# Pinning the VectorE sums of the modulation in the second to fourth token group of one encoder layer

## The chip, the cores and the metric

One Trainium2 chip, one of its cores. The metric is the device time of one execution in microseconds (us); lower is better. The time of a kernel is the median of several executions. A profile is one further execution, with its own time, recorded instruction by instruction. Five engines of the core work side by side, each on its own list of instructions in a fixed order: PE (TensorE, the matmuls), DVE (VectorE), ACT (ScalarE), POOL (GpSimd) and SP (SyncE), which here does nothing but issue DMAs. An engine that reaches an instruction whose input is not there waits, and all that stands behind it in its list waits too.

## The reference, cut to what matters

A layer of a streaming encoder runs over 2048 prompt tokens and 64 sample tokens of width 1024. Each of the two has its own conditioning vector, and the modulation `mod` is a product of that vector with a large weight:

```
mod = (c_act @ w_ada + b_ada)[:, None, :]
sh1, sc1, gt1, sh2, sc2, gt2 = jnp.split(mod, 6, -1)
h = rmsnorm(x, g1) * (1 + sc1) + sh1
proj = h @ w_in
...
hs, C, n, m = mlstm_seq(q..., k..., v..., ig, lf, C, n, m)
...
x = x + gt1 * mix
h2 = rmsnorm(x, g2) * (1 + sc2) + sh2
...
x = x + gt2 * ((jax.nn.silu(g) * a) @ w_down)
```

`sh2`, `sc2` and `gt2` (parts 3, 4 and 5 of the six) are wanted only after the mixer stage, so the kernel computes them in its background. This change concerns that background work.

## The kernel before

All inputs are float32. Where a full product is wanted, a number is split into a high and a low part, and three matmul passes replace one; the split weights of the first group are kept in memory (`hl_kept`) and loaded again by the later groups, 512 KB at a time.

The program has two stages. The first, about 0 to 740 us, is the mixer: four token groups of 512 tokens, the last with the 64 sample tokens besides. The second is the gated MLP in three groups of 704. For each of the four groups the mixer does this. `proj_v` (matmuls at L1141) makes V and the gates. `gate_rows` copies the gates out of PSUM (`gt`), transposes them on PE (L1184, L1185), and runs a chain of small rows over DVE and ACT: z, its absolute value, an Exp and an Ln on ACT, a log-sigmoid `lf`, two scans, then R and `RHL`. PE transposes these (L1238), DVE copies the result out as `CL`, PE multiplies (L1251), DVE copies out `GL`. Four heads follow, here hd0 to hd3. Each is three products q, k and the output gate th (`gemm`, matmuls at L492) and `lstm`: the decay factors (L1293) and their Exp on ACT (`at`), the transposes of k (L1306) that DVE multiplies into `kw`, the product of q and k (L1316) that DVE multiplies into `at`, the products of V with `kw` (L1331), which DVE adds into the states `st`, the cells (L1351, L1353), and `nd`. The stage ends with pooling (`poolmix`) and the output product (`outproj`).

Behind this lies background work that a generator hands out in small pieces between matmuls (`tick`):

- `ada(m, first)` (L191 to L228) computes one part of the modulation as plain sums on DVE. It has 16 steps. A step takes one 256 KB piece of `w_ada`, loaded by SP (L208) into a `raw` buffer, and adds it, multiplied by a column of the conditioning, into two rows of sums: one instruction for the prompt and one for the sample (L222 for the first of eight steps, L224 for the others). The sums are called `u` and `s` for the first eight steps and `s` and `acc` for the last eight. The load of step i+3 is issued when step i is done. The `raw` buffers are five in a ring, shared with the loads of other weights. `ada(2, True)` runs in the first group, and parts 3, 4 and 5 run in the second, third and fourth group with `first` false.
- `ada_end` (L230) finishes a part: a matmul (L234), a copy (L236), transposes (L240).
- `up_sums` prepares weights of the MLP: loads of `w_up` (L865), four DVE additions (L884, L885, L888, L889), a store of `wsum` (L875).
- `norm1` squares and adds the inputs of the next group (L930); `norm_h` makes the inputs of the MLP (L745 on DVE, L748 on ACT, load of `x2d` L758).

The order in each engine's list is not that of the source. A scheduler takes instructions that are ready in its own reckoning, by priority and by the place at which they were traced, so an instruction can float ahead of others that were traced before it. Two things bind it. Work called urgent (`gate_rows`, `lstm`, `poolmix`, and the splitting of weights at L425 and L428) has a raised priority. And `tc.keep_in_program_order(x)` pins an instruction: it may not stand ahead of what was traced before it on its engine. `up_sums` is pinned so in DVE's list and in SP's; the `w_ada` loads of the first group are pinned in SP's; the DVE steps of `ada` are not pinned at all.

Of the kernel before, what the change touches and what calls it, by code (L numbers as in the profile page):

```python
# [12 lines left out]
ALU = mybir.AluOpType  # L13
# [52 lines left out]
def tile_layer(ctx: ExitStack, tc: tile.TileContext, xT, vecs, cst, rst, w_mod, w_ada, w_qkou, w_v, w_pool,  # L66
               w_out, w_up, w_down, w_quad, st_C, st_pool, yT, o_pool, o_C, o_m, o_conv):
    nc = tc.nc
    act, dve, pool, pe = nc.scalar, nc.vector, nc.gpsimd, nc.tensor
# [105 lines left out]
    CA = cp.tile([P, KD, 2], F32, tag="CA", name="CA")  # L175
# [6 lines left out]
    def raw_tile():  # L182
        return wp.tile([P, WN], F32, tag="raw", name="raw", bufs=RB)
# [7 lines left out]
    def ada(m, first):  # L191


        todo = [(j, k) for j in range(2) for k in range(KD)]
        src = [w_ada[m - 2, k, :, j * 512:(j + 1) * 512] for j, k in todo]
        got = {}

        def load(i):
            if first:

                if i % 2 == 0 and i < len(todo):
                    w = a1.tile([P, 4, 256], F32, tag="w4", name="w4", bufs=4).rearrange("p (a b) c -> p a (b c)", a=2)
                    for d in range(2):
                        got[i + d] = w[:, d]
                        tc.keep_in_program_order(nc.sync.dma_start(out=w[:, d], in_=src[i + d]))
            elif i < len(todo):
                got[i] = raw_tile()[:, :512]
                nc.sync.dma_start(out=got[i], in_=src[i])  # L208
        lead = 4 if first else 3
        for i in range(lead):  # L210
            load(i)
        yield
        accs = []
        for i, (j, k) in enumerate(todo):
            if k == 0:

                acc = [a1.tile([P, UE], F32, tag=nm, name=nm)[:, :512] for nm in (("u", "s1"), ("s2", "acc"))[j]]
                accs += acc
            w = got.pop(i)
            for s in range(2):  # L220
                if k == 0:
                    dve.tensor_scalar(out=acc[s], in0=w, scalar1=CA[:, k, s:s + 1], scalar2=None, op0=ALU.mult)  # L222
                else:
                    dve.scalar_tensor_tensor(out=acc[s], in0=w, scalar=CA[:, k, s:s + 1], in1=acc[s],  # L224
                                             op0=ALU.mult, op1=ALU.add)
            load(i + lead)
            yield
        side.append(ada_end(m, accs))  # L228

    def ada_end(m, accs):  # L230

        pt = m2_ps()
        for c, acc in enumerate(accs):
            pe.matmul(pt[32 * c:32 * c + 32, :], ones[:, 0:32], acc, start=True, stop=True)  # L234
        MR = scr()
        dve.tensor_copy(MR[:, :512], pt)  # L236
        yield
        pt = m2_ps()
        for n in range(4):
            pe.transpose(pt[:, n * P:(n + 1) * P], MR[:, n * P:(n + 1) * P], ident)  # L240
        for j in range(2):
            bia = V[:, V_BA + m * 8 + 4 * j:V_BA + m * 8 + 4 * j + 4]
            dve.tensor_tensor(out=MOD[:, m, 4 * j:4 * j + 4],
                              in0=pt.rearrange("p (n c t) -> p n c t", n=4, c=4)[:, :, 2 * j:2 * j + 2, 0],
                              in1=bia.unsqueeze(2).broadcast_to([P, 4, 2]), op=ALU.add)
        if m == 4:
            scale_cols(G2, V_G2, 4, 0, KD)
# [139 lines left out]
    class Unit:  # L387

        state = 0
        w = raw = None  # L390
# [462 lines left out]
    if True:  # L853
# [604 lines left out]
        for o in groups:  # L1458
# [3 lines left out]
            if o.g > 0:  # L1462
                bg[3].append(ada(2 + o.g, False))
# [15 lines left out]
            if o.g == 0:  # L1479
                bg[3].append(ada(2, True))  # L1480
# [888 lines left out]
```

## Time and profile before

| what | us |
| --- | --- |
| median of 3 runs | 2169.86 |
| lowest and highest run | 2167.97, 2170.21 |
| the profiled execution | 2173.9 |
| its span, first to last instruction | 2172.1 |
| PE busy in the span | 2146.8 |
| DVE busy | 1663.1 |
| ACT busy | 1103.8 |
| PE busy in the first 800 us | 785.60 |
| the mixer of the second, third, fourth group begins at about | 205, 385, 566 |

In the views a row names an engine, a line of the program, an operation and its output and inputs (`out<-in`). A bracket holds the time for which the engine stood idle just before, and what ended that idle time. A view of waits adds these up by pair.

### The profile page before, as it was taken

The numbers are of one execution on the slowest core, as the hardware profiler recorded it, in microseconds if no ns is written. First come the engines' busy times: TensorE is split into PE (matmuls) and PEld (weight loads), VectorE is DVE, ScalarE is ACT, GpSimd is POOL, SyncE is SP. The second block draws the span as 40 slices with busy tenths as digits, with TensorE's granted clock in tenths as the row PEclk, the third lists the DMA queues.
The fourth block names the chain that finished last, engine by engine and source line by source line (L and its number), as shares of the span: only waits on it lengthen the run. The fifth ranks groups of instructions, "written<-read, shape, count | busy, mean of one in ns | idle before, by whom it ended". The sixth has DMA issues, their size and how long they took to land.

```text
span 2172.1 us, 38106 instructions
## 1 busy us (share of the span) xinstructions
PE 2146.8 (99%) x13529; PEld 2040.5 (94%) x13529; DVE 1663.1 (77%) x3107; ACT 1103.8 (51%) x2201; POOL 247.1 (11%) x468
## 2 busy tenths in 40 slices
PE   8999999999999999999999999999999999999998
PEld 7888888888899999999999999999999999999998
DVE  5768669767965778797968668888888797887874
ACT  4544335234333446464736445655656454565554
POOL 0000000001000201010101220100101121111112
PEclk9999999999999999999999999999999999999999
DMA  8986997997988477888969966666666875555542
GB/s 319 331 299 225 321 335 235 302 317 240 301 288 290 169 261 239 282 291 297 353 226 320 320 243 221 236 206 212 228 217 229 282 276 186 172 175 191 172 159 77
DMA packets 302439, 545.28 MB, mean 251 GB/s; under 512 B 25984, under 2 KB 118656, under 8 KB 302248
## 3 DMA queue, kind: packets, MB, share of 16 engines
q1 hardware_dynamic: 291656, 517.64, 70.3%
q10 hardware_dynamic: 10592, 25.20, 3.0%
q8 instruction: 107, 1.75, 0.3%
q14 instruction: 84, 0.69, 0.1%
HBM read 414.65 MB, written 128.08 MB: 250 GB/s over the span
## 4 chain that ended last, share of the span: by engine, by line
PE 84%; DMA 6%; DVE 5%; issue 2%; ACT 2%; SPq 0%; POOL 0%; DVEq 0%; ACTq 0%; POOLq 0%
PE mm L1602 35%; PE mm L492 21%; PE mm L2210 10%; PE mm L2071 9%; PE mm L1141 3%; DMA wt<-wsum 1%; DVE wt L428 1%; PE m L1331 1%; DMA hl_kept<-wt 1%; PE m L1316 1%; PE m L1351 1%; PE m L1353 1%; DMA raw<-w_ada 1%; DMA raw<-w_qkou 0%; DMA wsum<-w 0%
## 5 line engine op out<-in xcount | busy, mean ns | idle before, releaser
L1602 PE MATMUL mm<-hx,wt 128*128 128x352 f32 x5544 | 887.6, 321 | 1.1 <-DVE wt L428 0.7
L1602 PEld LDWEIGHTS mm<-hx,wt 128*128 128x128 f32 x5544 | 879.9, 188 | 3.6 <-DVE wt L428 2.4
L492 PE MATMUL mm<-hl,wt 128*128 128x512 f32 (+2 forms) x1920 | 385.4, 356 | 0.0
L425 ACT ACTIVATE wt<-raw 128x512 fp32r<-128x512 f32 (+3 forms) x468 | 275.9, 597 | 194.4 <-PE mm L492 56.1
L492 PEld LDWEIGHTS mm<-hl,wt 128*128 128x128 f32 x1920 | 314.7, 188 | 47.3 <-issue 4.4
L428 DVE TENSOR_TENSOR wt<-raw,wt 128x512 fp32r<-128x512 f32 (+3 forms) x468 | 306.9, 662 | 58.6 <-ACT wt L425 58.1
L2071 PE MATMUL mm<-av,wt 128*128 128x352 f32 x1512 | 248.2, 323 | 1.8 <-DVE x L2040 0.7
L2071 PEld LDWEIGHTS mm<-av,wt 128*128 128x128 f32 x1512 | 242.3, 188 | 5.1 <-DVE ea L1611 3.1
L2040 DVE SCALAR_TENSOR_TENSOR x<-mm,MOD,x 128x352 f32<-128x352 f32 (+5 forms) x384 | 180.1, 507 | 69.0 <-PE mm L2210 54.1
L2210 PE MATMUL mm<-av,wt 128*128 128x448 f32 (+1 forms) x1440 | 232.2, 322 | 0.0
L2210 PEld LDWEIGHTS mm<-av,wt 128*128 128x128 f32 x1440 | 221.1, 188 | 9.9
L1650 ACT ACTIVATE mm<-mm 128x352 f32<-128x352 f32 x204 | 91.4, 448 | 231.6 <-PE mm L1602 171.5
L492 PE MATMUL mm<-mx,wt 128*128 128x512 f32 (+1 forms) x960 | 182.9, 352 | 0.3 <-DVE scr L264 0.3
L492 PEld LDWEIGHTS mm<-mx,wt 128*128 128x128 f32 x960 | 159.4, 188 | 23.0 <-PE mm L492 0.5
L1580 DVE SCALAR_TENSOR_TENSOR ta<-ea,V,ta 128x704 f32<-128x704 f32 (+1 forms) x132 | 125.6, 951 | 54.1 <-ACT ta L1575 48.6
L1580 DVE SCALAR_TENSOR_TENSOR tg<-eg,V,tg 128x704 f32<-128x704 f32 (+1 forms) x132 | 125.6, 952 | 49.9 <-ACT tg L1575 47.3
L428 DVE TENSOR_TENSOR wt<-wt 128x512 fp32r<-128x512 f32 x204 | 138.1, 682 | 12.2 <-ACT wt L425 12.2
L425 ACT ACTIVATE wt<-wt 128x512 fp32r<-128x512 f32 x204 | 123.6, 622 | 37.4 <-DMA wt<-wsum 34.7
L1558 POOL COPY ea<-UC 128x2 f32<-128x2 f32 x66 | 33.0, 500 | 510.1 <-DVE ta L1580 428.7
L1799 ACT ACTIVATE tg<-tg 128x704 f32<-128x704 f32 (+1 forms) x66 | 52.4, 794 | 69.1 <-DVE tg L1580 69.0
L1141 PE MATMUL mm<-wt,hl 128*128 128x256 f32 (+1 forms) x576 | 71.2, 284 | 0.0
L1141 PEld LDWEIGHTS mm<-wt,hl 128*128 128x128 f32 x576 | 70.2, 189 | 0.8 <-issue 0.6
(306 smaller groups left out, 2214.6 us busy)
## 6 DMA issues: line engine op xcount, KB each, us to landing
wt<-wsplit SPq DMA_DIRECT2D x132, 512.0 KB, 4.3
raw<-w_up SPq DMA_DIRECT2D x198, 256.0 KB, 4.1
wt<-hl_kept SPq DMA_DIRECT2D x96, 512.0 KB, 5.8
wt<-wsum SPq DMA_DIRECT2D x132, 256.0 KB, 5.0
wsplit<-wt SPq DMA_DIRECT2D x66, 512.0 KB, 5.2
w<-w_up SPq DMA_DIRECT2D x88, 256.0 KB, 4.4
wsum<-w SPq DMA_DIRECT2D x44, 512.0 KB, 5.3
Bd<-fscr ACTq DMA_DIRECT2D x56, 352.0 KB, 4.2
```

What stands on the lines that cost most here:

```text
L425: act.activation(u.w[:, 0, :u.n], u.raw[:, :u.n], AF.Copy)
L428: dve.tensor_tensor(out=u.w[:, 1, :u.n], in0=u.raw[:, :u.n], in1=u.w[:, 0, :u.n].bitcast(F32), op=ALU.subtract)
L492: pe.matmul(ps[bi][:, :hi - lo], U[:, a, k % 4 * P:(k % 4 + 1) * P], mv[k][:, b, lo:hi], start=(at == 0 and pi == 0), stop=(k == order[-1] ...
L1141: pe.matmul(ps[ti][:n, :cols], h[4 * kh + k4][:, b, lo:lo + n], U[:, a, k4 % 2 * cols:(k4 % 2 + 1) * cols], start=(kh == 0 and k4 == 0 and ...
L1558: pool.tensor_copy(ext[:, 0:2], UC[:, f, :])
L1580: dve.scalar_tensor_tensor(out=t[:, :E], in0=ext[:, j:j + E], scalar=wc(j, f), in1=t[:, :E], op0=ALU.mult, op1=ALU.add)
L1602: pe.matmul(bk.t[:, :FH], U[:, a, kc * P:(kc + 1) * P], Bo.at(nm, kc, b), start=(first and kc == 0 and pi == 0), stop=(kc == 3 and pi == 2 ...
L1650: act.activation(to.t[:, :FH], bk.t[:, :FH], AF.Copy)
L1799: act.activation(self.tg[:, :E], self.tg[:, :E], AF.Silu)
L2040: dve.scalar_tensor_tensor(out=x3[n][:, a:b], in0=bk.t[:, a - lo:b - lo], scalar=gt2(n, s), in1=x3[n][:, a:b], op0=ALU.mult, op1=ALU.add)
L2071: pe.matmul(bk.t[:, :FH], U[:, a, c:c + P], quad.put(op, m, b), start=(first and m == 0 and pi == 0), stop=(m == 1 and pi == 2), skip_grou ...
L2210: pe.matmul(bks[i].t[:, :hi - lo], U[:, a, k % 4 * P:(k % 4 + 1) * P], av[k][:, b, lo:hi], start=(k == 0 and (a, b) == PASSES[0]), stop=(k ...
```

## The change

After it, each of the two DVE instructions of a step is pinned where `first` is false. That is 96 instructions, 32 in each of the three groups. No instruction is added or removed on any engine.

```diff
             for s in range(2):
                 if k == 0:
-                    dve.tensor_scalar(out=acc[s], in0=w, scalar1=CA[:, k, s:s + 1], scalar2=None, op0=ALU.mult)
+                    step = dve.tensor_scalar(out=acc[s], in0=w, scalar1=CA[:, k, s:s + 1], scalar2=None, op0=ALU.mult)
                 else:
-                    dve.scalar_tensor_tensor(out=acc[s], in0=w, scalar=CA[:, k, s:s + 1], in1=acc[s],
-                                             op0=ALU.mult, op1=ALU.add)
+                    step = dve.scalar_tensor_tensor(out=acc[s], in0=w, scalar=CA[:, k, s:s + 1], in1=acc[s],
+                                                    op0=ALU.mult, op1=ALU.add)
+                if not first:
+                    tc.keep_in_program_order(step)
             load(i + lead)
```

The lists of PE and POOL stay as they were, word for word. Those of DVE, SP and ACT change; in the pieces below lines behind L226 carry a number higher by two after the change.

**DVE, third group, hd0.** The rows from `CL` to `kw` before, with steps of `ada` (`s_4620`, `acc`) and of `up_sums` (`w_4688`) between them:

```order
L224 TENSOR_SCALAR acc<-raw,CA,acc 128x512
L264 COPY CL<-m_4557 128x4x4
L554 TENSOR_SCALAR RS_121<-m_4566 128x4
L224 TENSOR_SCALAR s_4620<-raw,CA,s_4620 128x512
L224 TENSOR_SCALAR acc<-raw,CA,acc 128x512
L264 COPY GL<-m_4614 128x16
L884 TENSOR_TENSOR w_4688<-w_4688 128x256
L224 TENSOR_SCALAR s_4620<-raw,CA,s_4620 128x512
L885 TENSOR_TENSOR w_4688<-w_4688 128x256
L224 TENSOR_SCALAR acc<-raw,CA,acc 128x512
L888 TENSOR_TENSOR w_4688<-w_4688 128x256
L264 TENSOR_TENSOR kw<-m_4647,CL 128x512
```

and the same place after:

```order
L266 COPY CL<-m_4557 128x4x4
L556 TENSOR_SCALAR RS_121<-m_4566 128x4
L224 TENSOR_SCALAR u<-raw,CA,u 128x512
L224 TENSOR_SCALAR s_4347<-raw,CA,s_4347 128x512
L886 TENSOR_TENSOR w_4492<-w_4492 128x256
...
L891 TENSOR_TENSOR w_4492<-w_4492 128x256
L224 TENSOR_SCALAR u<-raw,CA,u 128x512
L224 TENSOR_SCALAR s_4347<-raw,CA,s_4347 128x512
L266 COPY GL<-m_4614 128x16
L222 TENSOR_SCALAR s_4620<-raw,CA 128x512
L222 TENSOR_SCALAR acc<-raw,CA 128x512
L266 TENSOR_TENSOR kw<-m_4647,CL 128x512
```

Between `CL` and `kw` stood the thirteenth and fourteenth step before (each `s_4620` with `acc`), and there stand the seventh, eighth and ninth now.

**DVE, second group, hd1.** The last rows between the `nd` of hd0 and the `kw` of hd1, before:

```order
L930 TENSOR_TENSOR ssum<-ssum,mx_2640 128x512
L885 TENSOR_TENSOR w_2791<-w_2791 128x256
L224 TENSOR_SCALAR s_2810<-raw,CA,s_2810 128x512
L888 TENSOR_TENSOR w_2791<-w_2791 128x256
L224 TENSOR_SCALAR acc<-raw,CA,acc 128x512
L889 TENSOR_TENSOR w_2791<-w_2791 128x256
L930 TENSOR_TENSOR ssum<-ssum,mx_2640 128x512
L224 TENSOR_SCALAR s_2810<-raw,CA,s_2810 128x512
L224 TENSOR_SCALAR acc<-raw,CA,acc 128x512
L264 TENSOR_TENSOR kw<-m_3053,CL 128x512
```

and after:

```order
L224 TENSOR_SCALAR acc<-raw,CA,acc 128x512
L224 TENSOR_SCALAR s_2810<-raw,CA,s_2810 128x512
L224 TENSOR_SCALAR acc<-raw,CA,acc 128x512
L886 TENSOR_TENSOR w_2880<-w_2880 128x256
L932 TENSOR_TENSOR ssum<-ssum,mx_2640 128x512
L887 TENSOR_TENSOR w_2880<-w_2880 128x256
L890 TENSOR_TENSOR w_2880<-w_2880 128x256
L891 TENSOR_TENSOR w_2880<-w_2880 128x256
L224 TENSOR_SCALAR s_2810<-raw,CA,s_2810 128x512
L224 TENSOR_SCALAR acc<-raw,CA,acc 128x512
L224 TENSOR_SCALAR s_2810<-raw,CA,s_2810 128x512
L266 TENSOR_TENSOR kw<-m_3053,CL 128x512
```

In all there stand 4 instructions of `ada` and 4 of `up_sums` (and 3 of L930) between the two before, and 9, 8 and 3 now. The third group has the same numbers after the change, with none of `ada` before.

**SP, third group, the loads around hd0.** Before:

```order
L409 DMA wt<-hl_kept 128x2x512
L865 DMA w_4688<-w_up 128x2x256 x2
L208 DMA raw<-w_ada 128x512 x2
L409 DMA wt<-hl_kept 128x2x512 x2
L865 DMA w_4773<-w_up 128x2x256 x2
L208 DMA raw<-w_ada 128x512 x2
L409 DMA wt<-hl_kept 128x2x512 x3
L875 DMA wsum<-w_4539 512x1x256
```

and after:

```order
L867 DMA w_4601<-w_up 128x2x256 x2
L208 DMA raw<-w_ada 128x512
L867 DMA w_4688<-w_up 128x2x256
L208 DMA raw<-w_ada 128x512
L867 DMA w_4688<-w_up 128x2x256
L877 DMA wsum<-w_4492 512x1x256
L208 DMA raw<-w_ada 128x512 x2
L411 DMA wt<-hl_kept 128x2x512 x2
L867 DMA w_4773<-w_up 128x2x256 x2
L411 DMA wt<-hl_kept 128x2x512
```

A `w_ada` load whose buffer an earlier step must give back now stands nearer to the `hl_kept` loads that PE's weights come from. In the fourth group 15 of the 16 steps stood ahead of z before; after, the first stands in the end of `outproj`, and the rest behind z, on to hd1, so that the loads of `x2d` and the L745 and L748 rows change places there as well.

## The prediction

> **What bounds the kernel now.** The page comes first: its top and the row of PE.
>
> ```profile
> span 2172.1 us, 38106 instructions
> PE 2146.8 (99%) x13529; PEld 2040.5 (94%) x13529; DVE 1663.1 (77%) x3107; ACT 1103.8 (51%) x2201; POOL 247.1 (11%) x468
> ```
>
> PE works in 2146.8 of 2172.1 us. A change that only reorders DVE, ACT and SP can win no more than the idle time of PE that they cause where it acts, and can lose whatever new idle time it makes. So I asked the view of waits for PE, for the stretch from the second to the fourth group (190 to 740 us). It has two rows, each with what PE waited for, the sum, the count and the longest. The third row here is the longest of the whole execution.
>
> ```profile
> PE m L1331 <- DVE kw L264: 2.0, 1, 2.0
> PE m L1316 <- ACT at L264: 1.5, 1, 1.5
> PE m L1040 <- DMA mx<-xT: 5.7, 1, 5.7
> ```
>
> The first two are all that PE loses in those 550 us: 2.0 + 1.5 = 3.5 us, and that is the most that the change can win. The third lies at the very start, before PE's first matmul. Behind 740 us the lists of PE, DVE and SP are the same, and PE there only shifts with what came before.
>
> Next, the windows by stage (busy time and count of each engine, granted clock, DMA share, GB/s), to see how much room the other resources have:
>
> ```profile
> 260.00:320.00 60.00, 60.00 (x322) 50.61 (x321) 41.20 (x102) 20.29 (x64) 3.62 (x4) 1.00 0.97 336
> 390.00:440.00 50.00, 48.43 (x323) 43.59 (x321) 34.93 (x69) 14.54 (x29) 1.01 (x1) 1.00 0.95 325
> 440.00:500.00 60.00, 59.62 (x320) 50.38 (x321) 38.63 (x97) 20.71 (x64) 3.50 (x4) 1.00 0.91 305
> 605.00:660.00 55.00, 55.00 (x414) 52.45 (x413) 33.27 (x91) 20.76 (x62) 3.92 (x5) 1.00 0.87 282
> ```
>
> PE is full in each but for the 1.95 us around 440. DVE has a quarter to a third of its time free, so its sum is not the question, only the order in it. The DMA engines are nearly full (0.97 in hd0 and hd1 of the second group): a load that is issued late will land late.
>
> **The stall that the change touches.** Around 440 us the timeline of DVE and PE (start, length, instruction, and in brackets the idle time before it with its releaser):
>
> ```profile
> 429.69 0.75 DVE L224 SCALAR_TENSOR_TENSOR s<-raw,CA,s 128x512 f32<-128x512 f32 x1 [4.59 <-DMA raw<-w_ada]
> 431.02 0.17 DVE L264 COPY CL<-m 128x16 f32<-128x16 f32 x1
> 435.81 0.75 DVE L224 SCALAR_TENSOR_TENSOR s<-raw,CA,s 128x512 f32<-128x512 f32 x1 [4.55 <-DMA raw<-w_ada]
> 436.47 0.75 DVE L224 SCALAR_TENSOR_TENSOR acc<-raw,CA,acc 128x512 f32<-128x512 f32 x1
> 437.14 0.17 DVE L264 COPY GL<-m 128x16 f32<-128x16 f32 x1
> 439.55 0.68 DVE L264 TENSOR_TENSOR kw<-m,CL 128x512 f32<-128x512 f32 x1
> 440.38 1.13 PE L1331 MATMUL m<-va,kw 128*128 128x129 f32 x8 [1.95 <-DVE kw L264]
> 436.24 0.60 PE L1306 MATMUL m<-V,k 128*128 128x128 f32 x4
> ```
>
> Two steps of the sums, floated ahead of `CL` and `GL`, wait 4.59 and 4.55 us for their piece of `w_ada`, and hold DVE with them. `GL` comes at 437.14, five more rows follow, and `kw` starts at 439.55, though its input (L1306, 436.24 + 0.60) was there at 436.84. PE stands at L1331 from 438.43 to 440.38.
>
> **The change, part by part.** It adds and removes no instruction, so the work is the same 96 instructions; what changes is who stands in front of whom. A step is two instructions of 0.66 us each, by the starts of the rows at 435.81 and 436.47 (and 437.14 behind them), and an instruction of `up_sums` 0.33 us, by the starts of
>
> ```profile
> 273.76 0.42 DVE L884 TENSOR_TENSOR w<-w 128x256 f32<-128x256 f32 x1
> 274.09 0.69 DVE L930 TENSOR_TENSOR ssum<-ssum,mx 128x512 f32<-128x512 f32 x1
> 274.69 0.42 DVE L885 TENSOR_TENSOR w<-w 128x256 f32<-128x256 f32 x1
> ```
>
> which also give 0.60 for L930 (0.67 in the third group, where a row is 576 wide).
>
> *Third group, hd0.* With the pin the sums begin behind the gate chain's absolute value. Ahead of `CL` stand the sixth step instead of the eleventh and twelfth, ahead of `kw` the seventh to ninth. The pieces of the seventh and eighth were asked for three steps earlier, so I take them as landed. L1238's result is there at 428.36 + 0.60 = 428.96:
>
> ```profile
> 428.36 0.60 PE L1238 MATMUL m<-V,R 128*128 128x128 f32 x4
> ```
>
> From `CL` at that time to `kw` there are 6 instructions of the sums, 4 of `up_sums` and the two small copies: 6 x 0.66 + 4 x 0.33 + 0.3 = 5.6 us, which could start `kw` at 434.5; `GL`, which waits for PE's L1251, and the ninth step's piece move that to between 436.85 and 437.5. PE comes to L1331 at 438.43, and `kw` took 0.83 us from its start to L1331's. So the whole 1.95 us goes: **-1.95**. If a piece is again 4.5 us late here, the stall stays: 0.
>
> *Third group, hd1.* The rows that left hd0 must stand somewhere. Between `nd` of hd0 and `kw` of hd1 there are now 9 instructions of the sums, 8 of `up_sums` and 3 of L930: 5.94 + 2.64 + 2.0 = 10.6 us. What there was before:
>
> ```profile
> 450.29 0.69 DVE L264 TENSOR_TENSOR nd<-nd,sf 128x512 f32<-128x512 f32 x1 [1.12 <-POOL sf L1373]
> 459.73 0.69 DVE L264 TENSOR_TENSOR kw<-m,CL 128x512 f32<-128x512 f32 x1 [5.29 <-PE m L1306]
> ```
>
> From the end of `nd` (450.89) to `kw` lie 8.84 us, 5.29 of them idle. The new queue is 1.7 us longer than that, but `nd` comes earlier, since two of the four sums instructions that stood ahead of it (1.3 us) are gone and those ahead of `sf` with them. That leaves `kw` 0 to 0.8 us late if every piece is there, and the sixteenth step's piece, asked for when the thirteenth is done some 7 us before, is the one that may not be. I take **+0.5**, with ends 0 and 1.5.
>
> *Second group, hd0.* Before the change PE did not wait here; DVE did (a step held the fourth `gt`), but the gate chain had time to spare:
>
> ```profile
> 228.59 0.75 DVE L224 SCALAR_TENSOR_TENSOR u<-raw,CA,u 128x512 f32<-128x512 f32 x1 [3.21 <-DMA raw<-w_ada]
> 243.87 0.68 DVE L264 TENSOR_TENSOR RHL<-scr,RHL 4x512 fp32r<-4x512 f32 x1
> 250.33 0.60 PE L1238 MATMUL m<-V,R 128*128 128x128 f32 x4
> ```
>
> `RHL` was ready at 244.55, and PE transposes it at 250.33. Taking the 3.21 us wait out of the chain makes it earlier still, at no gain: 0.
>
> *Second group, hd1.* The same queue of 9, 8 and 3: 5.94 + 2.64 + 1.8 = 10.4 us.
>
> ```profile
> 265.97 0.75 DVE L224 SCALAR_TENSOR_TENSOR s<-raw,CA,s 128x512 f32<-128x512 f32 x1 [2.52 <-DMA raw<-w_ada]
> 272.55 0.69 DVE L264 TENSOR_TENSOR nd<-nd,sf 128x512 f32<-128x512 f32 x1 [0.90 <-POOL sf L1373]
> 279.55 0.69 DVE L264 TENSOR_TENSOR kw<-m,CL 128x512 f32<-128x512 f32 x1 [0.51 <-PE m L1306]
> 281.37 1.05 PE L1331 MATMUL m<-va,kw 128*128 128x129 f32 x8
> ```
>
> Four sums instructions stood between 265.97 and `nd`; without them `nd` starts at 272.55 - 4 x 0.66 = 269.9, ends at 270.5, and `kw` follows at 280.9. L1331 comes 0.83 later, 281.7, instead of 281.37: **+0.4**, with ends 0 and 1.2.
>
> *Fourth group.* Here the move is largest: 15 steps stood ahead of z, and now they run from z to hd1. The gate chain has room again: `RHL` was ready at 610.95 and PE took it at 618.80.
>
> ```profile
> 610.21 0.74 DVE L264 TENSOR_TENSOR RHL<-scr,RHL 4x576 fp32r<-4x576 f32 x1
> 618.80 0.71 PE L1238 MATMUL m<-V,R 128*128 128x128 f32 x5
> 621.58 0.43 DVE L884 TENSOR_TENSOR w<-w 128x256 f32<-128x256 f32 x1 [7.60 <-DMA w<-w_up]
> ```
>
> Of the eight steps that now stand between z and `CL`, those ahead of `RHL` replace others that stood ahead of z, and the later ones fall into the 7.60 us for which DVE had nothing to do; that wait of L884 for `w_up`, ahead of `CL` before, moves behind the sums. The one PE stall there:
>
> ```profile
> 682.20 0.59 DVE L745 SCALAR_TENSOR_TENSOR mx<-mx,G,mx 128x352 f32<-128x352 f32 x1 [3.62 <-DMA mx<-x2d]
> 683.90 1.31 ACT L264 ACTIVATE at<-m,CL 128x128 f32<-128x128 f32 x5
> 685.10 1.42 PE L1316 MATMUL m<-q,k 128*128 128x128 f32 x10 [1.55 <-ACT at L264]
> ```
>
> L745 waits 3.62 us for `x2d`, ACT's L748 waits for it, and `at` stands behind L748. After the change three fewer pairs of L745 and L748 are done by then, one L745 stands ahead of `kw` in place of one ahead of `at`, and the `x2d` load is still behind `up_sums` loads on SP. The stall may go (-1.55), stay, or come back as a wait for `kw` that takes the whole 3.62 (+2.1). I take the middle, **0**.
>
> *Sum.* -1.95 + 0.5 + 0.4 + 0 = -1.05 us against the profiled execution's own 2173.9 us (its span 2172.1 and 1.8 around it), hence 2172.85. That execution is 4.0 us slower than the median of 2169.86; the same difference on the median gives **2168.8 us**. The ends: all lower ones, -1.95 - 1.55 = -3.5, give 2166.4; all upper ones, 0 + 1.5 + 1.2 + 2.1 = +4.8, give 2174.7.
>
> **The rivals.** *First, SP's queue.* A `w_ada` load can only be issued when its buffer is given back by an earlier step; on SP it stands ahead of `hl_kept` loads, now with more steps still open.
>
> ```profile
> DMA to landing us min/median/max: 3.5/5.8/8.7
> SPq L208 <- DVE wt L428: 7.5, 10, 2.1
> ```
>
> The first row is for the 96 `hl_kept` loads, the second for what SP has waited in the `w_ada` loads so far: 10 times, never above 2.1 us. One such load feeds 12 matmuls, 2.7 to 3.0 us of PE by
>
> ```profile
> 261.60 2.47 PE L492 MATMUL mm<-hl,wt 128*128 128x512 f32 x10
> ```
>
> By the order after, I place two `hl_kept` loads of the third group behind steps that end some 9 and 7 us before PE wants the weights: with 5.8 us of landing there are 1 to 3 us to spare, with 8.7 none. If pieces come 4.6 us late as at 429.69, each of these costs up to 3 us of PE, and two or three of them 6 to 9: **2176 to 2179**, against -1 from the rest about 2177. For it: the DMA share of 0.97 and 0.91 in hd0 and hd1. Against it: PE did not wait once for `hl_kept` before, though SP waits ten times. It decides from a hold of about 2 us on.
>
> The Trainium skill, "TensorE: Matmul & The Clock Gate", in the part on the HAM clock gate, says that an idle window of about 3.4 us takes the array's clock to half, and that it needs as long a busy window to return; by that each wait above 3.4 us would cost up to another 1.7 us (an estimate from that page), and such a rival 2180. No wait of PE before reaches 3.4 us apart from the 5.7 us at the very start, and the rows above grant 1.00 in every stretch, so this trace can't bear it out; I leave it a small part of this rival.
>
> *Second, both stalls go and no new one comes:* -3.5, **2166.4**. For it: in hd1 the queue ends within a microsecond of the time wanted. Against it: L745 has the same late load.
>
> *Third, the change wins nothing:* a step of `w_ada` or of `up_sums` blocks in front of `kw` in the third group again, and the stall stays or moves to hd1; 0, **2169.9**. For it: pinning does not make a load land, and 24.1 us of DVE's idle time ended with `raw<-w_ada`, 12 times:
>
> ```profile
> DMA raw<-w_ada: 24.1, 12
> ```
>
> **How the numbers follow.** I give the forecast 0.40, both stalls gone 0.10, no gain (within a microsecond or two of 2169.9, small new waits among it) 0.20, SP's queue or another late load in front of PE 0.30. About 0.2%, 4.3 us, is what a measurement of this kernel tells from no change. Faster by more needs more than the 3.5 us there are, so it is left 0.05, half of the case with both stalls gone. Slower by more is the last case whole, and 0.02 of the third: 0.32. The rest, 0.63, is within. The range takes in the lower end (2166.4, with a little beneath it) and reaches up into the last case: 2166.0 to 2177.0; the likeliest case's own is 2166.4 to 2174.7.
>
> **What would show it.** Right: in the third group no L1331 row waits for `kw` in hd0, and no L224 ahead of `CL` or `GL` waits 4 us; in hd1 of the second and third group `kw` follows an L224 without idle time, with L1331 at most 1 us late. The fourth group shows whether L1316 still waits for `at`, or L1331 for `kw` instead. Wrong, by SP: the view of waits has rows of PE L492 for DMA `wt<-hl_kept`. Wrong, by DVE: an L224 ahead of `kw` waits several us for `w_ada` and PE waits with it. If PE's waits between 190 and 740 sum to more than 8 us, the mechanism that I put at 0.30 was the likely one.

## The result, and the profile after

| | before | after |
|---|---|---|
| median of 21 runs | 2172.91 us | 2175.58 us |
| profiled execution, its own time | 2173.9 us | 2173.41 us |
| its span | 2172.1 us | 2171.6 us |
| PE busy | 2146.8 us | 2147.0 us |

The ratio after to before is 1.0016 with an interval of 1.0010 to 1.0022 (here and below a 95% interval): about 3.5 us slower. That is inside the band of 0.2% that the prediction called no change, but with this many runs it is plainly on the slower side. The 2169.86 us that the forecast started from was a median of three runs; the median over the 21 runs shown here is 3 us higher, which moves the time but not the ratio.

The pair of profiled executions hides the loss, since the one after the change has the shorter span. The offset of the same PE row, after minus before, shows why. All these are PE rows of the timeline after the change; the rows of before that are set against them are in the prediction, except the one of hd1 in the fourth group; the row at 457.82, hd1 of the third group, is there for its wait.

```profile
247.62 0.60 PE L1240 MATMUL m<-V,R 128*128 128x128 f32 x4
279.05 1.16 PE L1333 MATMUL m<-va,kw 128*128 128x129 f32 x8 [0.25 <-DVE kw L266]
436.04 1.05 PE L1333 MATMUL m<-va,kw 128*128 128x129 f32 x8
457.82 1.16 PE L1333 MATMUL m<-va,kw 128*128 128x129 f32 x8 [0.50 <-DVE kw L266]
615.16 0.71 PE L1240 MATMUL m<-V,R 128*128 128x128 f32 x5
656.60 1.95 PE L1318 MATMUL m<-q,k 128*128 128x128 f32 x10 [4.67 <-ACT at L266]
687.64 1.31 PE L1318 MATMUL m<-q,k 128*128 128x128 f32 x10
```

In before the row of hd1 is this one:

```profile
655.41 0.83 PE L1316 MATMUL m<-q,k 128*128 128x128 f32 x6
```

The offsets are 247.62 - 250.33 = -2.7 in hd0 of the second group, where the change has done nothing to PE yet (ten of the twelve profiles taken after that of before stand 1.7 to 2.7 us earlier than it at this row, so it was the execution of before that was late there), 279.05 - 281.37 = -2.3 in hd1, 436.04 - 440.38 = -4.3 in hd0 of the third group, 615.16 - 618.80 = -3.6 at the start of the fourth, 656.60 - 655.41 = +1.2 in its hd1 and 687.64 - 685.10 = +2.5 in its hd2. From the first row to the last the change costs 5.2 us: it wins 1.6 up to hd0 of the third group, gives 0.7 back by the fourth, and loses 6.2 in the fourth.

PE's waits from 190 to 740 us, after the change (releaser, sum, count, longest):

```profile
PE m L1318 <- ACT at L266: 4.7, 1, 4.7
PE m L1333 <- DVE kw L266: 0.7, 2, 0.5
```

The waits of before were 2.0 us for `kw` and 1.5 for `at`; now there is one of 4.7 for `at`, at another place. Behind it PE is slowed too. The windows after the change (start and end, length, busy time and count of PE, PEld, DVE, ACT and POOL, granted clock, DMA share, GB/s):

```profile
652.00:656.60 4.60, 0.00 (x1) 0.01 (x1) 2.94 (x8) 2.26 (x7) 0.00 (x0) 1.00 0.98 314
656.60:658.00 1.40, 1.40 (x8) 1.25 (x8) 1.40 (x4) 0.61 (x2) 0.00 (x0) 0.72 0.96 321
658.00:664.00 6.00, 6.00 (x24) 3.42 (x24) 4.54 (x10) 1.57 (x3) 0.33 (x2) 0.50 1.03 357
664.00:668.00 4.00, 4.00 (x32) 3.76 (x31) 1.81 (x7) 0.67 (x3) 0.00 (x0) 0.99 0.74 216
```

From 657.2 to 664.0 the granted clock is 0.50, and PE does 24 matmuls in 6 us where it does 32 in the 4 us behind. By the offsets this costs 2.5 - 1.2 + 1.55 = 2.9 us (1.55 is the wait of before in hd2 that is gone).

**Where the 4.7 us come from.** DVE in the fourth group's hd1, then ACT, in the timeline after the change:

```profile
645.44 2.05 DVE L747 SCALAR_TENSOR_TENSOR mx<-mx,G,mx 128x352 f32<-128x352 f32 x4
653.14 0.42 DVE L886 TENSOR_TENSOR w<-w 128x256 f32<-128x256 f32 x1 [5.65 <-DMA w<-w_up]
653.49 0.58 DVE L747 SCALAR_TENSOR_TENSOR mx<-mx,G,mx 128x352 f32<-128x352 f32 x1
...
654.10 0.59 ACT L750 ACTIVATE mx<-mx,MOD 128x352 f32<-128x352 f32 x1 [5.38 <-DVE mx L747]
...
655.42 1.30 ACT L266 ACTIVATE at<-m,CL 128x128 f32<-128x128 f32 x5
```

An addition of `up_sums` waits 5.65 us for its block of `w_up`; L747 stands behind it on DVE, L750 waits for L747, and `at` stands behind L750 on ACT. Nothing here is a step of `ada`. Its block was asked for late. SP's `w_up` loads after the change:

```profile
596.40 0.55 SPq L867 DMA_DIRECT2D w<-w_up  x1
616.14 1.25 SPq L867 DMA_DIRECT2D w<-w_up  x2
618.60 1.20 SPq L867 DMA_DIRECT2D w<-w_up  x2
627.87 1.20 SPq L867 DMA_DIRECT2D w<-w_up  x2
638.01 1.20 SPq L867 DMA_DIRECT2D w<-w_up  x2
648.92 1.20 SPq L867 DMA_DIRECT2D w<-w_up  x2
```

and before:

```profile
597.61 2.01 SPq L865 DMA_DIRECT2D w<-w_up  x2
607.22 1.20 SPq L865 DMA_DIRECT2D w<-w_up  x2
616.81 1.21 SPq L865 DMA_DIRECT2D w<-w_up  x2
629.74 1.22 SPq L865 DMA_DIRECT2D w<-w_up  x2
632.72 1.25 SPq L865 DMA_DIRECT2D w<-w_up  x2
639.43 1.20 SPq L865 DMA_DIRECT2D w<-w_up  x2
```

Where before a pair of loads (x2, one block) goes out at 598, 607 and 617, after there is none from 597 to 616. A `w_up` load needs a block's additions and store done, and the additions stood still. DVE at the start of the fourth group, after the change:

```profile
585.14 0.16 DVE L266 COPY gt<-m 64x8 f32<-64x8 f32 x1 [1.27 <-PE m L1143]
591.70 0.74 DVE L266 TENSOR_SCALAR scr<-m,V 4x512 f32<-4x512 f32 x1 [6.40 <-PE m L1187]
...
606.30 0.42 DVE L886 TENSOR_TENSOR w<-w 128x256 f32<-128x256 f32 x1
```

and before:

```profile
583.50 0.42 DVE L884 TENSOR_TENSOR w<-w 128x256 f32<-128x256 f32 x1
```

Before, DVE filled the time ahead of the gate chain with sums and additions. Now the steps of `ada` may not pass the gate chain, and the additions, which are pinned too, may not pass the steps: DVE stands empty for 6.40 us until PE delivers the chain's first input, and the additions that ran at 583.5 run at 606.3.

That the gap makes the load at 648.92 late is not shown by these rows. The pairs can be counted from the first in both executions, and set against PE, which stands 3.6 us earlier than before there. The 35th, right behind the gap, is 12.6 us late (616.14 against 607.22), the 37th is 1.8 us late (627.87 against 629.74), and the 39th is 13.1 us late (648.92 against 639.43). So most of the gap had been made up, and then a load came late anew. That one stands behind the landing of a store of `wsum` that was issued at 640.56 and took 8.3 us to land; before, the store of the same count was issued at 634.03 and took 5.4 us.

**Where the gain came from.** DVE in the third group's hd0, after the change:

```profile
431.80 0.17 DVE L266 COPY GL<-m 128x16 f32<-128x16 f32 x1 [0.39 <-PE m L1253]
...
434.71 0.69 DVE L266 TENSOR_TENSOR kw<-m,CL 128x512 f32<-128x512 f32 x1 [1.95 <-PE m L1308]
```

No step waits for its piece ahead of `GL` or `kw`, `kw` waits for PE and not PE for `kw`, and the stall of 1.95 us is gone. In the whole execution after the change no step of the second to fourth group waits for its piece any more; before, those of L224 held DVE for 24.1 us.

### The profile page after: what moved, and what is told of

Its sections match the earlier page's. It is cut to its first block, busy times and chain, and to the rows that moved or that the text cites. A ratio compares the mean times of both kernels' runs of the same rounds, so it can differ in the third digit from the quotient of the medians.

```text
span 2171.6 us, 38123 instructions
## 1 busy us (share of the span) xinstructions
PE 2147.0 (99%) x13529; PEld 2040.5 (94%) x13529; DVE 1665.7 (77%) x3107; ACT 1104.4 (51%) x2201; POOL 246.9 (11%) x468
## 4 chain that ended last, share of the span: by engine, by line
PE 87%; DVE 6%; DMA 3%; issue 2%; ACT 2%; POOL 0%; SPq 0%; ACTq 0%; DVEq 0%; POOLq 0%
PE mm L1604 36%; PE mm L494 22%; PE mm L2212 10%; PE mm L2073 9%; PE mm L1143 3%; DVE wt L430 1%; PE m L1333 1%; PE m L1353 1%; PE m L1318 1%; PE m L1355 1%; DVE tg L1582 1%; ACT tg L1577 0%; PE mm L1079 0%; DMA wsum<-w 0%; DMA wt<-dsum 0%
## 5 line engine op out<-in xcount | busy, mean ns | idle before, releaser
L494 PE MATMUL mm<-hl,wt 128*128 128x512 f32 (+2 forms) x1920 | 386.6, 357 | 0.1
L494 PEld LDWEIGHTS mm<-hl,wt 128*128 128x128 f32 x1920 | 315.6, 189 | 48.5 <-issue 5.3
L494 PE MATMUL mm<-mx,wt 128*128 128x512 f32 (+1 forms) x960 | 182.9, 353 | 0.2 <-DVE scr L266 0.2
L494 PEld LDWEIGHTS mm<-mx,wt 128*128 128x128 f32 x960 | 159.3, 188 | 22.9 <-PE mm L494 0.4
```

The costliest lines, as they stand in the source:

```text
L494: pe.matmul(ps[bi][:, :hi - lo], U[:, a, k % 4 * P:(k % 4 + 1) * P], mv[k][:, b, lo:hi], start=(at == 0 and pi == 0), stop=(k == order[-1] ...
```

## The experiments

Kernels are compared with runs of before on the same chip. The theory on which the first ones rest: the pins of the second and third group win a little, those of the fourth lose more, by one wait of PE and the halved clock behind it.

**Pins in the second and third group alone.**

```diff
-                if not first:
+                if not first and m < 5:
```

> The pin in the second and third group alone, the fourth group's sums free as before. Theory (the loss comes from the fourth group's hd1: late additions for the MLP weights ahead of the decay factors, then a halved clock): no PE wait above 2 us between 190 and 740, the 1.95 us wait for kw in the third group gone, 0.4 to 0.7 us of new waits for kw in hd1 of the second and third group, the 1.55 us wait at about 683 still there, clock 1.00 throughout; 1.0 to 1.5 us faster than before, ratio 0.9993 to 0.9996. Rival (the pin costs in each group): slower than before by 1 us or more, ratio above 1.0004.

Measured: 2169.82 us, ratio 0.9991 (0.9982 to 1.0000). A second time, with other kernels beside it:

> The pin in the second and third group alone once more, whether it is really faster than before: ratio 0.9988 to 0.9997 and below 1 with its interval when taken with the first eleven runs; if it is no faster, 1.0000 or above.

Measured: 2170.98 us, ratio 0.9983 (0.9974 to 0.9992). So this part of the change makes the kernel faster, by 0.1 to 0.2%, and of the versions tried it beats both before and the change. PE's waits from 190 to 740 us in the first of the two profiles:

```profile
PE m L1318 <- ACT at L266: 1.3, 1, 1.3
PE mm L494 <- DMA wt<-hl_kept: 0.8, 1, 0.8
PE m L1333 <- DVE kw L266: 0.2, 1, 0.2
```

2.3 us in all instead of 3.5. The second profiled execution took 2176.11 us of its own, against its kernel's median of 2170.98, and had two waits of 1.2 and 1.7 us in hd2 of the fourth group, with a halved clock for 3.4 us behind them.

**Pins in the third group alone.**

```diff
-                if not first:
+                if m == 4:
```

> The pin in the third group alone. Theory: the 1.95 us wait for kw in hd0 of the third group is gone, about 0.6 comes in hd1, none in the second group, the fourth as before: ratio 0.9985 to 0.9998, within 1 us of the pin in the second and third group. Rival (the gain of the second and third group together comes from the second, in a way that the profiles do not show): 1.0000 or above.

Measured: 2172.73 us, ratio 0.9991 (0.9982 to 1.0001). The waits are 0.7 for `hl_kept` and 0.5 for `at`. The gain is of the same size as with the second group's pins added; the intervals don't tell the two apart.

**Pins in the fourth group alone.**

```diff
-                if not first:
+                if m == 5:
```

> The pin in the fourth group alone. Theory: the third group's 1.95 us wait for kw is back, the fourth group's hd1 has a PE wait of 4 to 5 us for the decay factors with DVE idle 5 us ahead of it for a w_up load, then 6 to 7 us at a granted clock of 0.50, and the 1.55 us wait at 683 is gone: 4.7 + 3 - 1.6 = about 6 us slower than before, ratio 1.0025 to 1.003. Rival (the pin costs in each group about the same): 1 to 2 us slower, ratio below 1.001, and no stretch at half clock.

Measured: 2175.73 us, ratio 1.0014 (1.0006 to 1.0023): slower by itself, though less than expected. The mechanism is the same, at the same place, with a shorter wait (an addition of `up_sums` waits 3.9 us for `w_up`; PE in the timeline):

```profile
655.87 1.44 PE L1318 MATMUL m<-q,k 128*128 128x128 f32 x5 [2.92 <-ACT at L266]
```

A window of this execution:

```profile
656.00:662.00 6.00, 6.00 (x25) 3.53 (x25) 4.46 (x11) 2.05 (x4) 0.00 (x0) 0.50 0.92 321
```

Here the old wait for `kw` is back in the third group, as it should be, with 1.7 us.

**The change again**, for a second profile.

> The changed kernel as it is, for a second profile of it and for times on the same chip as the others. Theory: PE waits 4 to 5 us for the decay factors in hd1 of the fourth group again and runs at half clock for about 7 us behind it; ratio 1.0012 to 1.002. Rival (that stall was one execution's): the wait is absent or in another place, with the same ratio.

Measured: 2175.27 us, ratio 1.0015 (1.0006 to 1.0024). The wait recurs, with 5.3 us, and the halved clock lasts longer, some 10 us:

```profile
656.00:660.00 4.00, 1.97 (x8) 1.78 (x8) 3.45 (x10) 2.39 (x8) 0.00 (x0) 0.61 0.92 266
660.00:667.00 7.00, 7.00 (x29) 4.46 (x28) 4.01 (x8) 1.57 (x3) 0.33 (x2) 0.50 0.90 319
```

So neither the wait nor the halved clock is a freak of one execution. This one has a span of 2176.5 us, 4.4 above that of before.

**First and last eight steps of the fourth group.** Each half pinned by itself, with the pins of the second and third group kept:

```diff
-                if not first:
+                if not first and (m < 5 or j == 0):
```

> All pinned but the last eight steps of the fourth group. Theory: the additions stand as in the kernel before in hd1 (no sums between nd and them), their loads come earlier, and PE waits less than 2 us there, clock 1.00; like the pin in the second and third group alone, ratio 0.9988 to 1.0000. Rival (the first eight steps, in the gate chain, are what delays the additions): wait of 3 us or more and half clock, ratio 1.001 or above.

Measured: 2179.10 us, ratio 1.0026 (1.0016 to 1.0036).

```diff
-                if not first:
+                if not first and (m < 5 or j == 1):
```

> All pinned but the first eight steps of the fourth group. Theory: order in hd1 as in the changed kernel, six sums instructions and a block of additions more behind nd; PE waits 3 to 5 us, half clock for 7 us or more, ratio 1.001 to 1.002. Rival (the first eight steps are the cause): no wait above 2 us, clock 1.00, ratio 0.9988 to 1.0000.

Measured: 2174.10 us, ratio 1.0004 (0.9995 to 1.0013). The kernel without pins in the fourth group, measured beside these two on the same chip, had 2170.98 us. Against it the pins of the first eight steps cost 8 us and those of the last eight 3, so most of the loss comes with the first eight, and not all of it. What the last eight cost is not explained: in that profile PE's waits from 190 to 740 us sum to 2.4 us, the clock is whole, and by the offsets PE loses nothing between hd0 of the second group (-2.3) and 740 us (-2.7).

With the first eight pinned, the `w_up` loads have the same gap, in SP's timeline:

```profile
596.64 1.57 SPq L867 DMA_DIRECT2D w<-w_up  x1
598.90 0.55 SPq L867 DMA_DIRECT2D w<-w_up  x1
618.98 1.25 SPq L867 DMA_DIRECT2D w<-w_up  x2
```

With the last eight pinned there is none:

```profile
595.12 2.54 SPq L867 DMA_DIRECT2D w<-w_up  x2
605.87 1.21 SPq L867 DMA_DIRECT2D w<-w_up  x2
614.24 1.20 SPq L867 DMA_DIRECT2D w<-w_up  x2
```

and no wait of PE above 1.2 us. But with the first half pinned the wait was not in hd1 for `at`; it was in hd2, 4.2 us for `kw`, with DVE's L747 waiting 3.8 and 5.9 us for `x2d`. The theory of both runs, that the loss comes with the last eight steps, was wrong; the rival of the first run was right about the wait, the clock and the ratio. What comes late with the pins is more than one load, and which one PE meets first varies with the order behind.

**Holding the additions back in hd1.** If the addition that waits for `w_up` is the whole cause, keeping `up_sums` out of that stretch should win the loss back.

```diff
-    quiet = []
+    quiet, hold = [], []
...
-            if at in ups and not quiet:
+            if at in ups and not quiet and not hold:
                 tick(4)
...
         def proj_qko(o, h, q=None):
+            late = hold[:]
+            hold.clear()
...
             th = a2.tile([P, TMAX], F32, tag="th", name="th")
+            hold[:] = late
...
             for hd in range(NH):
+                hold[:] = [1] if o.last and hd == 1 else []
                 qko = proj_qko(o, h, q1)
+                hold.clear()
```

> The changed kernel, all 96 steps pinned, but the additions for the MLP weights (up_sums) get no turn during the output-gate product of hd1 in the fourth group, so that one block of four additions less stands ahead of the decay factors there; the nine sums instructions stay where they are. Theory (DVE waits for the w_up load of that last block, ACT's rows wait for DVE, the decay factors for ACT, PE for them): the block now in that place has its load long since, so PE's 4.7 us wait and the stretch at half clock are gone, and with the gain of the third group kept it runs 1 to 3 us faster than before, ratio 0.9985 to 0.9996. Rival (the pinned sums themselves, 9 instructions of 0.66 us, fill DVE and delay the rows): the wait stays at 3 to 5 us, half clock too, ratio 1.001 to 1.002.

Measured: 2179.13 us, ratio 1.0022 (1.0012 to 1.0032). The wait in hd1 is gone, and one as long has come in hd2: DVE, then PE, in the timeline of this kernel.

```profile
689.83 0.58 DVE L747 SCALAR_TENSOR_TENSOR mx<-mx,G,mx 128x352 f32<-128x352 f32 x1 [8.61 <-DMA mx<-x2d]
...
691.07 0.87 DVE L266 TENSOR_TENSOR kw<-m,CL 128x512 f32<-128x512 f32 x2
...
691.79 0.47 PE L1390 MATMUL m<-V,nd 128*128 128x128 f32 x1 [5.00 <-DVE kw L266]
```

This is the stall that the prediction weighed at +2.1, at L747 ahead of `kw`, with 5.00 us of PE in place of the 3.62 weighed there. The last load of `x2d` was issued at 684.5 in the change and at 684.0 here, against 677.4 before; in the change L747 waits 4.6 us for `x2d` in hd2 too, but PE, delayed in hd1 by then, does not wait there.

**Leaving out stores of `wsum`.** In SP's waits of the change from 636 to 664 us the loads of `w_up` stand behind stores that have not landed:

```profile
SPq L867 <- DMA wsum<-w: 11.6, 3, 5.7
```

So eight blocks' stores were taken out of the fourth group (and as many added earlier, to keep the rest of the program).

```diff
-                    pin(nc.sync.dma_start(out=wsum[f, :, :, c:c + 256], in_=w))
+                    n = 2 * f + c // 256
+                    if not 28 <= n < 36:
+                        pin(nc.sync.dma_start(out=wsum[f, :, :, c:c + 256], in_=w))
+                    if 12 <= n < 20:
+                        pin(nc.sync.dma_start(out=wsum[f + 8, :, :, c:c + 256], in_=w))
```

> The changed kernel, all 96 steps pinned, but eight blocks of the additions (the 29th to 36th, those of the fourth group) are not stored when they are made; other blocks' sums are stored in their place earlier, in the second and third group, so the weights of these blocks are wrong in the MLP and the work there is the same. What is left out is the wait of a w_up load for the landing of a store. Theory (the stores' landing, 6 to 8 us each behind the 20 us hole, makes the w_up loads late, DVE waits for them, and PE): DVE's wait for w_up ahead of L747 in hd1 is gone, PE waits less than 2 us in hd1 and no half clock follows there, ratio 0.9980 to 1.0000. Rival (the loads are late for another cause, the pinned steps or DMA traffic): PE waits 3 us or more there with half clock, ratio above 1.001.

Measured: 2181.03 us, ratio 1.0029 (1.0015 to 1.0043), but by the offsets 5.5 us were lost ahead of the fourth group already (-1.8 in hd0 of the second, +3.7 at the start of the fourth). In the third group, among the added stores, PE waits four times for `hl_kept`, 2.8 us in all, and PE's own rows stand in another order. So the time of this run says little; its waits say more. In hd1 DVE no longer waits for `w_up` and PE no longer stands; so there the landing of the stores was what made the load late. In hd2 PE then waits 4.7 us for `kw`, with DVE in front of it:

```profile
691.26 0.58 DVE L747 SCALAR_TENSOR_TENSOR mx<-mx,G,mx 128x352 f32<-128x352 f32 x1 [10.06 <-DMA mx<-x2d]
```

Twice, then, the first late load was taken away, and the next one took its place.

**Starting the fourth group's steps later**, behind the projection of `va`, all of them pinned:

```diff
-            if o.g > 0:
+            if o.g > 0 and not o.last:
                 bg[3].append(ada(2 + o.g, False))
...
                 va = proj_v(o, h, cols)
+                if o.last:
+                    bg[3].append(ada(2 + o.g, False))
```

> The changed kernel, all 96 steps pinned, but in the fourth group the sums are begun only after proj_v, so that no pinned step is traced ahead of the block of additions that belongs there. In all kernels so far that lost, SP issues no w_up load for about 20 us (596 to 616 in the changed kernel), since the additions at about 583 stand behind pinned steps that wait for the gate chain and come at 606; in all that did not, there is a load at about 605. Theory (that hole makes later w_up and x2d loads late, DVE waits for one of them ahead of L747, and PE with it): a w_up load between 600 and 612, no PE wait above 2.5 us in hd1 or hd2 of the fourth group, no half clock, ratio 0.9980 to 1.0000. Rival (the pinned steps among hd0 and hd1 of the fourth group cost by themselves): waits of 3 us or more, half clock, ratio above 1.001.

Measured: 2176.24 us median, but a ratio of 1.0003 with an interval from 0.9993 to 1.0013: no difference from before can be told. The gap in the `w_up` loads is shorter, from 597 to 611, and the wait in hd1 is gone, as expected. Not as expected, PE waits once in the fourth group, 3.8 us in hd2, behind an addition that waits 2.86 for `w_up`, and the clock is halved for 3.4 us.

**Keeping PE busy in hd1.** L1295's matmul is issued 17 times at that place, so that PE does not stand idle while it waits for `at`. The work done is the same.

```diff
-                pe.matmul(pr[:n, :w], E_r[:, hd, :n], RHL[:, lo:lo + w], start=True, stop=True)
+                for _ in range(17 if o.last and hd == 1 and a == 0 else 1):
+                    pe.matmul(pr[:n, :w], E_r[:, hd, :n], RHL[:, lo:lo + w], start=True, stop=True)
```

> The changed kernel with the matmul of the decay factors of hd1 in the fourth group issued 17 times in place of once (the same product into the same place), about 3.6 us of PE work that nobody needs, just ahead of the place where PE waits. Theory: the wait for the decay factors is set by DVE and ACT, not by PE, so L1318 starts as late as before, PE's idle time there falls from 4.7 to about 1 us, the granted clock stays 1.00, and the 3 us that the halved clock cost come back: some 3 us faster than the changed kernel, ratio to before 1.0000 to 1.0006. Rival (the halved clock costs nothing, or comes whatever PE does there): as slow as the changed kernel or up to 3.6 us slower, ratio 1.0016 to 1.0033.

Measured: 2176.09 us, ratio 1.0019 (1.0010 to 1.0027). The repeated matmuls took 4.07 us, PE's wait in hd1 is gone (one of 1.4 us comes in hd2), and the clock stayed whole:

```profile
652.00:664.00 12.00, 11.24 (x80) 9.04 (x79) 9.73 (x23) 4.55 (x11) 0.33 (x2) 1.00 0.90 301
```

The time did not get better. In the profiled execution PE has lost 4.0 us against before from hd0 of the second group to 740 us, against 5.1 and 7.1 in the two profiles of the change; the medians show nothing of it (2176.09 against 2175.27 for the change beside it). So that the halved clock comes from the wait is borne out by this one profile, but that it costs the whole kernel its 3 us is not. Behind 740 us the two profiles of the change get some of their lateness back, 3.4 us (+2.5 in hd2, -0.9 at PE's last rows) and about 1 us. If how much comes back depends on how late PE is, that would explain it; it was not tried.

## Why the prediction was right or wrong

- *Third group, hd0, -1.95:* right. The rows give -4.3 - (-2.3) = -2.0, `kw` waits for L1308 and not for a piece, and it starts at 434.71 + 2.3 = 437.0 by the clock of before, inside the 436.85 to 437.5 that was worked out.
- *Second group, hd1, +0.4, and third, +0.5:* right. -2.3 - (-2.7) = +0.4, and the wait of 0.50 at 457.82 is the second; `kw` follows an L224 without idle time in both.
- *Second group, hd0, 0:* right, as -2.7 stays up to L1333.
- *Fourth group, 0:* this is the step that failed: "The stall may go (-1.55), stay, or come back as a wait for `kw` that takes the whole 3.62 (+2.1). I take the middle, **0**." In the profile after the change it measured about +6.2: +4.8 for a new wait for `at` in hd1, +2.9 for the halved clock behind it, -1.6 for the old stall in hd2, which did go. Only one place was priced, the one where before had shown a stall. The sentence ahead of it noted that the wait of L884 for `w_up` "moves behind the sums", and counted that as free since it had been free where it stood. But the additions are pinned themselves, so a pinned step that waits for the gate chain holds them, their stores and their next loads. The order behind z should have been followed on SP as far as the rows L747 in hd1.
- *First rival, SP's queue, 2176 to 2179:* the time came near it (2175.58), but by luck. The loss is 3.5 us and not the 6 to 9 of this rival; the other 3 us are those by which the median of before is higher than the 2169.86 it was counted from. Its mechanism did not come true either: in the change no PE L494 waits for `hl_kept`; what came late was `w_up`, through DVE and ACT. The last phrase of the case, "another late load in front of PE", covers it, but its test, waits of PE above 8 us in all between 190 and 740, did not come true: they sum to 5.4, against 3.5 before, and most of the rest of the loss in this profile is the clock.
- *The halved clock:* the rule of the Trainium skill ("TensorE: Matmul & The Clock Gate", the HAM clock gate) was given only a small part of a rival, because no wait of before between 190 and 740 us reached 3.4 us. The trace agrees with the rule that an idle PE is followed by a clock of 0.50, in stretches of some 3.4 us, and not with the idle time that it asks for: 2.92 us of wait sufficed. The halved clock lasted two such stretches after the change (657.2 to 664.0) and three in its second profile.
- *Second and third rival:* both stalls of before did go, but with a new one; the third did not happen, as `w_ada` pieces no longer hold DVE ahead of `CL`, `GL` or `kw`.
- *Sum:* without the fourth group the terms give -1.05 us, 0.9995. The pins of the second and third group alone measured 0.9991, with 0.9995 inside its interval, and 0.9983, with 0.9995 above its interval: as forecast or better. The loss lies in the fourth group.
- *Three readings that are off, without effect on the sum:* by the four windows DVE has 30 to 40% of its time free, not a quarter to a third. The 0.97 of the DMA engines belongs to the second group; in the third, which the first rival is about, the windows have 0.95 and 0.91. And the row `SPq L208 <- DVE wt L428` counts only the waits that one line ended; all waits of SP in the `w_ada` loads from 190 to 740 us are 32, 22 us in all, still none above 2.1.

What stays open is why the loads of both `w_up` and `x2d` end up as late as they do. The gap goes with the loss in most of the kernels, but no run moved the gap alone, and in the change most of it had been made up before the load that PE came to wait for. Open too are the 3 us that the last eight steps cost, and what gives lateness back behind 740 us.

## What to carry to other kernels

Pinning floated work pays where that work stood, waiting for its load, ahead of rows that PE needs (here the second and third group, 0.1 to 0.2%). It lost in the fourth group, where another pinned stream stands behind it: ask of each such stream what its last step releases, and follow the transfers to the first row that PE waits for, group by group and not only where the old stall was. A new wait of 2 to 5 us on an otherwise full PE can bring a halved clock, which in the two profiles of the change was another 3 to 4 us of PE; the run that avoided it was no faster by its median, so that price is shown for PE's rows and not for the whole kernel.

## What the hardware showed that was not expected

The halved clock came after shorter waits and lasted longer than I had thought. Beside waits of PE of 2.2 us (at 105 us, for `w_out`, in the kernel that holds the additions), 2.9, 3.8, 4.2, 4.7, 5.0 and 5.3 us the granted clock was 0.50 for 3.4, 6.8, 3.4, 6.8, 6.8, 6.8 and 10.2 us, all near a multiple of 3.41. The halved stretch began 0.6 us after the wait's end in the change (657.2 against 656.6) and 1.2 us ahead of it in its second profile. Two waits of 1.2 and 1.7 us within 8 us of each other were followed by 3.4 us of it as well. The two single waits of 2.0 us in before (at 105 and 440 us) and that of 1.4 us in the kernel with the repeated matmuls had none. Neither the threshold nor the length follows from the length of the wait alone: two waits of 4.7 us, one in the change and one without the stores, had 6.8 and 3.4 us behind them.
